# Half of the second gate's adaLN steps ahead of the second norm, their broadcast inside it, and three small first transfers on ScalarE's queue

## The chip, the core and the metric

The kernel runs on one core of one Trainium2 chip. A core has five engines, each with an instruction stream of its own that it works through in order: TensorE (PE in the profile; its weight loads are PEld), VectorE (DVE), ScalarE (ACT), GpSimd (POOL) and SyncE (SP). Transfers are started by an engine's queue and carried by 16 DMA engines. PE is granted one of two clocks, 1.2 or 2.4 GHz; the profile's PEclk is the granted share of the higher one. The metric is the time of one execution on the device in microseconds (us).

## What is computed

One layer of a hybrid decoder block on 256 tokens of width 2048 in float32. A conditioning vector c gives six modulation vectors (a shift, a scale and a gate for each half of the layer):

```python
c_act = jax.nn.silu(c)
mod = c_act @ w_ada[l] + b_ada[l]                   # (2048) x (2048, 6 * 2048)
sh1, sc1, g1, sh2, sc2, g2 = [...]                  # six pieces of 2048
xn = _rmsnorm(h, norm1_g[l]) * (1.0 + sc1) + sh1
proj = xn @ w_in[l]                                 # q, k, v, g_ret, conv gates, merge gates
y_ret = (retention(rotary(q), rotary(k), v) * jax.nn.silu(g_ret)) @ w_ret_o[l]
y_conv = (bg * _causal_dwconv(cg * xc, w_sc[l])) @ w_conv_o[l]
gate_a, gate_b = jnp.split(jax.nn.sigmoid(gate_logits + b_gate[l]), 2, axis=-1)
h = h + g1 * ((gate_a * y_ret + gate_b * y_conv) @ w_mix_o[l])
xn2 = _rmsnorm(h, norm2_g[l]) * (1.0 + sc2) + sh2
gt = _causal_dwconv(xn2 @ w_gate[l], w_ffconv[l], b_ffconv[l])
h = h + g2 * ((jax.nn.silu(gt) * (xn2 @ w_up[l])) @ w_down[l])
return _rmsnorm(h, final_g)
```

The gate g2 is used only at the very end of the layer, by the residual after w_down. The shift and scale of the second norm and the gate g1 are wanted before it.

## The kernel before

All weights stream from memory once, in tiles of 512 KB (256 rows x 512 columns). The program is one list of units, `units`, worked through by the loop at the end of `tile_trunk_block`. A unit has up to three steps, which the loop calls at different distances: `load` starts its transfer 9 units ahead (LOAD_AHEAD), `prep` runs 2 units ahead (PREP_AHEAD; 4 in the first stage), `run` issues its products. The kinds of unit:

- **Weights** (L285): `load` brings a raw tile (ring of 7, on SP's queue, L295); `prep` casts it to a rounded half `hi` on ACT (L307) and subtracts to get the low half `lo` on DVE (L308); in the first stage some go to tiles called `hw` and `lw`. `run` issues the products: three per tile and token half in `x_block` (activations stationary, L379 with hi, L380 with lo, L381 with hi), or in `w_block` (weights stationary) a 512-wide product with hi (L412) and a 256-wide one with lo (L417).
- **Ada** (L313): one step of adaLN, the product of c_act with w_ada, done on DVE and not on PE: `load` brings 512 KB of w_ada through the same raw ring, `prep` multiplies it by one number per partition and adds it to an accumulator `ada` (L342 the first of an accumulator, L344 the others). After 16 such steps half a modulation vector is summed but for the partitions; `done` sums them with a product with ones, and stores it.
- **Call** and **Loaded**: other work, and small loads with a step that uses them (the merge gates' bias among them, added at L706).

`spread` (L509) deals Ada units evenly among the Weights units of a stage. Which Ada units go where is set by counts: ADA_QK to each half of the q/k blocks, ADA_CONV0 to each half's convolution block, ADA_RET to w_ret_o, ADA_CONV to the later convolutions, ADA_OUT to w_conv_o, and what is left of `ada_mid` to w_mix_o. `ada_ff` holds the 32 steps of gate 2: 26 go to the first feed-forward blocks, 6 to the second block of the first w_down pass.

Order in time: the start (x's norm, its transposes L247 with copies L251, scales L358 to L370, first modulated activations L449 and L92) up to 32 us; the first stage, which interleaves chunks of xn and the first modulation, to about 400; q/k blocks, retention and the first convolution for two pairs of heads each, to 750; w_ret_o to 845; convolutions to 976; w_conv_o to 1075; w_mix_o to 1166; norm2 to 1178; the feed-forward blocks and w_down to the end.

A scheduler orders each engine's instructions; behind the first stage, DVE's L308 and L344 are held to the order of the program. `broadcast` (L541) turns half an accumulated gate into a tile of all partitions: two products of a matrix of ones with 512 columns each (L546), and two copies on ACT (L548). `norm2` (L882) ends the token norm: it sums the squares (L884), takes the root on POOL (L222), builds two diagonal tiles `dr` (L888), transposes the last quarter of h (`turn_h(3)`, L857, copies L860) and multiplies ones by the diagonals (L891).

## Time and profile before

| | us |
|---|---|
| median of 3 runs | 1919.06 (1918.51 to 1920.63) |
| the profiled execution, its own time | 1921.2 |
| its span | 1919.4 |
| PE busy | 1873.3 (98% of the span) |
| DVE busy | 1386.4 (72%) |
| ACT busy | 890.5 (46%) |
| mean granted clock of PE | 0.994 |

PE is busy nearly all the time, so the page's part 4 (the chain of work that ended last) lies on PE almost throughout. What is not PE's own work shows as its waits: in a timeline a row ends with the idle time before it and what ended that. Rows count the duration of each instruction; PE's products overlap one another, so in a row of products the time from one start to the next is what counts. A duration beside "x4" is that of the four together.

### The profile page before, as it was taken

The page shows a single profiled execution, that of the slowest core. Times are in us where ns is not written, and L with a number is a line of the kernel's source. Part 1 is how long each engine was busy: PE and PEld are TensorE (multiplying, and loading weights), DVE is VectorE, ACT ScalarE, POOL GpSimd, SP SyncE. Part 2 cuts the span into 40 slices and gives each one's busy share as a digit, 9 for nine tenths or more (in the row PEclk, how much of TensorE's full clock was granted, in tenths as well). Part 3 has the DMA queues.
Part 4 walks back from the last instruction along what each step waited for, and adds up shares of the span by engine and source line. Part 5 has one row for each costly group of instructions (what it writes and reads, how often), then busy time and mean ns, then how long its engine had stood idle before and what let it go on. Part 6 is the DMA issues. An engine that isn't in the chain of part 4 may idle for free.

```text
span 1919.4 us, 25328 instructions
## 1 busy us (share of the span) xinstructions
PE 1873.3 (98%) x9543; PEld 1579.5 (82%) x9543; DVE 1386.4 (72%) x1638; ACT 890.5 (46%) x1150; POOL 21.7 (1%) x51
## 2 busy tenths in 40 slices
PE   5999999999999999999999999999999999999997
PEld 5788888888888887888877787888888888888886
DVE  6799996766777787668777766877776556666665
ACT  4643434534444544344444445555554335555543
POOL 1000000000000000000000000000000000000000
PEclk9999999999999999999999999999999999999999
DMA  8989996566777676877777874777776756666553
GB/s 291 308 280 307 313 326 186 183 198 197 234 256 226 213 252 237 270 267 265 272 253 252 296 273 135 258 245 239 240 248 205 244 194 189 191 192 209 187 196 111
DMA packets 222093, 452.90 MB, mean 236 GB/s; under 512 B 14933, under 2 KB 27537, under 8 KB 221585
## 3 DMA queue, kind: packets, MB, share of 16 engines
q1 hardware_dynamic: 220768, 448.99, 70.8%
q10 hardware_dynamic: 720, 2.10, 0.3%
q8 instruction: 75, 1.23, 0.3%
q14 instruction: 50, 0.40, 0.1%
q0 software_dynamic: 480, 0.18, 0.0%
HBM read 449.11 MB, written 2.10 MB: 235 GB/s over the span
## 4 chain that ended last, share of the span: by engine, by line
PE 91%; DVE 4%; issue 2%; DMA 1%; ACT 1%; POOL 0%; SPq 0%; POOLq 0%; DVEq 0%; ACTq 0%
PE acc L412 30%; PE acc L417 15%; PE acc L380 15%; PE acc L381 14%; PE acc L379 14%; DVE lo L308 1%; PE misc L358 1%; DMA ld<-in_b_gate 1%; DMA raw<-in_w_ada 1%; PE misc L247 0%; DVE ada L344 0%; PE misc L546 0%; PE misc L632 0%; DVE conv L751 0%; ACT junk L228 0%
## 5 line engine op out<-in xcount | busy, mean ns | idle before, releaser
L307 ACT CAST hi<-raw 128x1024 fp32r<-128x1024 f32 (+1 forms) x601 | 623.9, 1038 | 862.8 <-PE acc L412 433.4
L308 DVE TENSOR_TENSOR lo<-raw,hi 128x1024 fp32r<-128x1024 f32 (+1 forms) x601 | 718.1, 1204 | 335.1 <-ACT hi L307 334.8
L412 PE MATMUL acc<-xn,hi 128*128 128x512 f32 x2688 | 840.6, 397 | 1.8 <-DVE xn L902 1.8
L417 PEld LDWEIGHTS acc<-xn,lo 128*128 128x128 f32 x2688 | 498.4, 188 | 124.2 <-DVE lo L308 10.1
L417 PE MATMUL acc<-xn,lo 128*128 128x256 f32 x2688 | 524.7, 279 | 3.6 <-DVE lo L308 3.3
L412 PEld LDWEIGHTS acc<-xn,hi 128*128 128x128 f32 x2688 | 414.7, 189 | 7.2 <-DVE xn L902 2.6
L344 DVE SCALAR_TENSOR_TENSOR ada<-raw,c_act,ada 128x1024 f32<-128x1024 f32 (+2 forms) x199 | 238.5, 1198 | 0.5
L379 PE MATMUL acc<-hi,ff_t 128*128 128x512 f32 x332 | 129.6, 390 | 0.0
L380 PE MATMUL acc<-lo,ff_t 128*128 128x512 f32 x332 | 129.3, 389 | 0.0
L381 PE MATMUL acc<-hi,ff_t 128*128 128x512 f32 x332 | 129.2, 389 | 0.0
L379 PE MATMUL acc<-hi,xn 128*128 128x512 f32 x304 | 119.5, 397 | 4.1 <-ACT xn L92 2.4
L380 PE MATMUL acc<-lo,xn 128*128 128x512 f32 x304 | 120.2, 395 | 1.1 <-DVE lo L308 1.1
L381 PE MATMUL acc<-hi,xn 128*128 128x512 f32 x304 | 119.5, 394 | 0.0
L381 PE MATMUL acc<-hw,xn 128*128 128x512 f32 x208 | 82.0, 394 | 0.0
L380 PE MATMUL acc<-lw,xn 128*128 128x512 f32 x208 | 81.8, 393 | 0.0
L379 PE MATMUL acc<-hw,xn 128*128 128x512 f32 x208 | 81.1, 395 | 0.0
L307 ACT CAST hw<-raw 128x1024 fp32r<-128x1024 f32 (+1 forms) x58 | 55.6, 959 | 45.0 <-DMA raw<-in_w_in 22.6
L423 ACT COPY sb<-acc 128x256 f32<-128x256 f32 x168 | 61.8, 368 | 30.9 <-PE acc L417 28.8
L380 PEld LDWEIGHTS acc<-lo,ff_t 128*128 128x128 f32 x332 | 62.3, 188 | 13.5 <-issue 0.2
L379 PEld LDWEIGHTS acc<-hi,ff_t 128*128 128x128 f32 x332 | 62.3, 188 | 13.0 <-ACT hi L307 0.2
L381 PEld LDWEIGHTS acc<-hi,ff_t 128*128 128x128 f32 x332 | 62.3, 188 | 12.9
L379 PEld LDWEIGHTS acc<-hi,xn 128*128 128x128 f32 x304 | 57.4, 189 | 17.8 <-ACT xn L92 2.4
(192 smaller groups left out, 1768.9 us busy)
## 6 DMA issues: line engine op xcount, KB each, us to landing
raw<-in_w_in SPq DMA_DIRECT2D x272, 512.0 KB, 4.8
raw<-in_w_ada SPq DMA_DIRECT2D x160, 512.0 KB, 4.9
raw<-in_w_gate SPq DMA_DIRECT2D x88, 512.0 KB, 4.3
raw<-in_w_up SPq DMA_DIRECT2D x88, 512.0 KB, 4.2
raw<-in_w_down SPq DMA_DIRECT2D x88, 512.0 KB, 4.4
raw<-in_w_ret_o SPq DMA_DIRECT2D x32, 512.0 KB, 5.3
raw<-in_w_conv_o SPq DMA_DIRECT2D x32, 512.0 KB, 5.5
raw<-in_w_mix_o SPq DMA_DIRECT2D x32, 512.0 KB, 5.5
```

Source lines behind the costliest of these rows:

```text
L307: nc.scalar.copy(self.hi, self.raw)
L308: in_order(nc.vector.tensor_tensor(self.lo, self.raw, self.hi.bitcast(F32), op=ALU.subtract))
L344: in_order(nc.vector.scalar_tensor_tensor(acc, self.raw[:, k], c_act[:, kt:kt + 1], acc, op0=ALU.mult, op1=ALU.add))
L358: nc.tensor.matmul(ps[:, i:i + 1], lhsT=flat[:, (s0 + i) * P:(s0 + i + 1) * P], rhs=ones[:, 0:1], start=True, stop=True,)
L379: nc.tensor.matmul(ps, lhsT=xh, rhs=u.hi[:, k, :], start=k0 + k == first, stop=False)
L380: nc.tensor.matmul(ps, lhsT=xh, rhs=u.lo[:, k, :], start=False, stop=False)
L381: nc.tensor.matmul(ps, lhsT=xl, rhs=u.hi[:, k, :], start=False, stop=k0 + k == end - 1)
L412: nc.tensor.matmul(ps, lhsT=u.hi[:, k, i * P:(i + 1) * P], rhs=xt(k0 + k).rearrange("p h s -> p (h s)"), start=k0 + k == 0, stop=False,)
L417: nc.tensor.matmul(ps[:, 0:S], lhsT=u.lo[:, k, i * P:(i + 1) * P], rhs=xt(k0 + k)[:, 0, :], start=False, stop=last and k == UK - 1,)
L423: nc.scalar.copy(b, ps[:, S:2 * S])
```

## The change

- The counts become 8, 12, 15, 28 and 14 instead of 6, 11, 13, 24 and 12, and `ada_mid` gets the 16 steps of gate 2's first half behind its 96: 97 of 112 are dealt before w_mix_o instead of 83 of 96, and 15 instead of 13 are left for w_mix_o.
- `ada_ff` keeps the 16 steps of the second half; all go to the first feed-forward blocks, none to w_down.
- When the first half is summed, `gate2_done` only keeps its accumulator; `norm2` issues its broadcast, behind the diagonal tiles and ahead of `turn_h(3)`, into two banks of the ring `acc` instead of `misc`.
- The three small transfers that stand first in the program (c, 8 KB; the positions, 128 KB to all partitions; the rotary frequencies, 0.5 KB) are started by ScalarE's queue instead of SyncE's. On ACT the first stands ahead of the table load, the others behind it; on SP the two 1 MB transfers of x are now first.

```diff
--- before.py
+++ after.py
@@ -38,7 +38,7 @@
 ROT_AT = 24
 DEFER_SG = 2
 ROT_EARLY = 12
-ADA_QK, ADA_CONV0, ADA_RET, ADA_CONV, ADA_OUT = 6, 11, 13, 24, 12
+ADA_QK, ADA_CONV0, ADA_RET, ADA_CONV, ADA_OUT = 8, 12, 15, 28, 14
 LAST_HEAD = 2
 NORM_AHEAD = 4
 
@@ -108,11 +108,11 @@
 
     x_tok = blk8("x_tok0", [P, D], F32), blk8("x_tok1", [P, D], F32)
     vec0 = w4("vec0", [P, P])
-    nc.sync.dma_start(vec0[0:16, :], c[0].rearrange("(r k) -> r k", k=P))
+    nc.scalar.dma_start(vec0[0:16, :], c[0].rearrange("(r k) -> r k", k=P))
     pos_i = small.tile([P, S], I32, tag="sb", name="pos_i")
-    nc.sync.dma_start(pos_i, positions.to_broadcast([P, S]))
+    nc.scalar.dma_start(pos_i, positions.to_broadcast([P, S]))
     ivf = const.tile([P, 1], F32, name="ivf")
-    nc.sync.dma_start(ivf, inv_freq)
+    nc.scalar.dma_start(ivf, inv_freq)
     for t in range(2):
         nc.sync.dma_start(x_tok[t], x[t * P:(t + 1) * P, :])
 
@@ -551,7 +551,9 @@
         return lambda acc: broadcast(acc, g1b, half, "g1b", misc_bank)
 
     def gate2_done(half):
-        return lambda acc: broadcast(acc, g2b, half, "g2b", misc_bank)
+        if half:
+            return lambda acc: broadcast(acc, g2b, 1, "g2b", misc_bank)
+        return lambda acc: g2b.update(acc=acc)
 
     def vec_done(which, half):
         def done(acc):
@@ -573,7 +575,8 @@
         ada_mid += ada_units(4, half, vec_done("scale", half))
     for half in range(2):
         ada_mid += ada_units(2, half, gate1_done(half), True)
-    ada_ff = [u for half in range(2) for u in ada_units(5, half, gate2_done(half), True)]
+    ada_mid += ada_units(5, 0, gate2_done(0), True)
+    ada_ff = ada_units(5, 1, gate2_done(1), True)
 
     def take(extra, n):
         got = extra[:n]
@@ -886,6 +889,7 @@
         dr = w4("dr", [P, 2, P])
         for t in range(2):
             nc.vector.tensor_scalar_mul(dr[:, t, :], ident, r[:, t:t + 1])
+        broadcast(g2b["acc"], g2b, 0, "g2b", acc_bank)
         turn_h(3)
         row["t"] = acc_bank()[:, 0:S]
         nc.tensor.matmul(row["t"], lhsT=ones, rhs=dr.rearrange("p t n -> p (t n)"), start=True, stop=True)
@@ -1023,7 +1027,7 @@
     for b0, b1_, final in ((0, cut, False), (cut, NB, True)):
         seq = [u for j in range(b0, b1_) for u in ff_blocks(j)]
         if not final:
-            seq = seq[:8] + spread(seq[8:], take(ada_ff, 26))
+            seq = seq[:8] + spread(seq[8:], take(ada_ff, 16))
             for k0 in range(KT - 2, NORM_AHEAD - 1, -2):
                 seq.insert((k0 - NORM_AHEAD) // 2 + 1, Call((lambda k: lambda: normed(k, k + 2))(k0)))
         units += seq
```

Lines of the changed kernel are 2 to 4 higher than those of before: L618 is L621, L860 is L863, L901 is L905.

How it moves instructions: on ACT in the first stage, where the last quarter of the second token half is copied (`x_t`), the first modulated activations are made (L449, `xn` at L92) and the first weights cast. Before:

```order
L251 COPY x_t_168<-misc_205 128x512
L251 COPY x_t_168<-misc_211 128x512
L307 CAST hi_304<-raw_268 128x1024
L449 ACTIVATE x_t_167<-x_t_167,b_218,a_217 128x256 x2
L92 CAST xn_29_221<-x_t_167 128x2x256
L307 CAST hw_316<-raw_282 128x1024
L307 CAST hi_339<-raw_302 128x1024
L480 COPY v_tok_225<-acc_352 128x512
L480 COPY v_tok_225<-acc_353 128x512
L307 CAST hw_348<-raw_311 128x1024
```

and now:

```order
L251 COPY x_t_168<-misc_205 128x512
L307 CAST hi_304<-raw_268 128x1024
L251 COPY x_t_168<-misc_211 128x512
L449 ACTIVATE x_t_167<-x_t_167,b_218,a_217 128x256 x2
L307 CAST hw_316<-raw_282 128x1024
L92 CAST xn_29_221<-x_t_167 128x2x256
L307 CAST hi_339<-raw_302 128x1024
L307 CAST hw_348<-raw_311 128x1024
L480 COPY v_tok_225<-acc_352 128x512
```

`hi_304` has moved ahead of the last copy of x_t, `hw_316` ahead of the cast of xn, and `hw_348` ahead of the first two copies of v_tok.

On DVE at the end of the first q/k block, where the four additions of the block's results (`qk`) stand; `lo_3510` before and `lo_3542` now are the low half of the next block's first unit. Before:

```order
L308 TENSOR_TENSOR lo_3464<-raw_3327,hi_3463 128x1024
L308 TENSOR_TENSOR lo_3486<-raw_3344,hi_3485 128x1024
L308 TENSOR_TENSOR lo_3510<-raw_3376,hi_3509 128x1024
L618 TENSOR_TENSOR qk_3519<-acc_3350,sb_3517 128x256
L618 TENSOR_TENSOR qk_3519<-acc_3351,sb_3525 128x256
L618 TENSOR_TENSOR qk_3519<-acc_3352,sb_3532 128x256
L618 TENSOR_TENSOR qk_3519<-acc_3353,sb_3539 128x256
L308 TENSOR_TENSOR lo_3545<-raw_3398,hi_3544 128x1024
```

and now:

```order
L308 TENSOR_TENSOR lo_3464<-raw_3327,hi_3463 128x1024
L308 TENSOR_TENSOR lo_3470<-raw_3344,hi_3469 128x1024
L344 SCALAR_TENSOR_TENSOR ada_3186<-raw_3376,c_act,ada_3186 128x1024
L621 TENSOR_TENSOR qk_3516<-acc_3350,sb_3514 128x256
L621 TENSOR_TENSOR qk_3516<-acc_3351,sb_3522 128x256
L621 TENSOR_TENSOR qk_3516<-acc_3352,sb_3529 128x256
L621 TENSOR_TENSOR qk_3516<-acc_3353,sb_3536 128x256
L308 TENSOR_TENSOR lo_3542<-raw_3398,hi_3541 128x1024
```

The adaLN step has taken the place of a unit of weights ahead of the additions, and the next block's first low half has come behind them.

On ACT in norm2, with the two last sums of squares (L228), the copies of the last quarter of h (`h_t`) and the first activations of the feed-forward stage. Before:

```order
L307 CAST hi_9945<-raw_9811 128x1024
L228 ACTIVATE junk_9852,ss_h<-h_tok_9072 128x512
L228 ACTIVATE junk_9863,ss_h<-h_tok_9074 128x512
L860 COPY h_t_9764<-misc_9877 128x512
L860 COPY h_t_9764<-misc_9883 128x512
L901 ACTIVATE xn_1948_9893<-u_9894,b_220 128x256
```

and now:

```order
L307 CAST hi_10003<-raw_9862 128x1024
L228 ACTIVATE junk_9903,ss_h<-h_tok_9123 128x512
L548 COPY g2b_9928<-acc_9929 128x512
L228 ACTIVATE junk_9914,ss_h<-h_tok_9125 128x512
L548 COPY g2b_9928<-acc_9932 128x512
L863 COPY h_t_9815<-misc_9935 128x512
L863 COPY h_t_9815<-misc_9941 128x512
L905 ACTIVATE xn_1968_9951<-u_9952,b_220 128x256
```

One copy of the broadcast (`g2b`) stands behind each of the two sums of squares, so the first of them ahead of the second sum, and both ahead of the copies of h.

## Rows read from the trace of the kernel before

**Rows 1.** Page, part 4: the chain that ended last, share by engine.

```profile
PE 91%; DVE 4%; issue 2%; DMA 1%; ACT 1%; POOL 0%; SPq 0%; POOLq 0%; DVEq 0%; ACTq 0%
```

**Rows 2.** PE's waits: line, what it waited for: us, times, longest.

```profile
PE acc L380 <- DVE lo L308: 5.3, 5, 2.6
PE acc L417 <- DVE lo L308: 3.3, 6, 1.2
```

**Rows 3.** Timeline of the start: start, us, engine, line, operation, tiles, count [idle].

```profile
0.74 0.39 SPq L111 DMA_DIRECT2D vec<-in_c  x1
...
2.12 0.91 SPq L117 DMA_DIRECT2D x_tok<-in_x  x2
...
2.60 0.25 PE L121 MATMUL misc<-ident,vec 16*128 16x16 f32 x1 [2.60 <-DMA vec<-in_c]
...
7.47 0.42 DVE L145 TENSOR_TENSOR rotary_room<-rotary_room,a_hi 128x256 f32<-128x256 f32 x1
...
9.44 0.63 ACT L228 ACTIVATE junk<-x_tok 128x512 bf16<-128x512 f32 x1 [6.12 <-DMA x_tok<-in_x]
...
12.92 0.49 DVE L342 TENSOR_SCALAR ada<-raw,c_act 128x512 f32<-128x512 f32 x1 [3.97 <-DMA raw<-in_w_ada]
...
19.21 9.07 PE L247 MATMUL misc<-diags,x_tok 128*128 128x128 f32 x56 [0.90 <-DVE diags L240]
...
28.32 0.59 ACT L251 COPY x_t<-misc 128x512 f32<-128x512 f32 x1 [0.35 <-PE misc L247]
...
28.81 1.05 ACT L307 CAST hi<-raw 128x1024 fp32r<-128x1024 f32 x1
...
31.54 0.61 DVE L342 TENSOR_SCALAR ada<-raw,c_act 128x768 f32<-128x768 f32 x1
...
32.37 0.79 PE L379 MATMUL acc<-hi,xn 128*128 128x512 f32 x1 [2.35 <-ACT xn L92]
```

**Rows 4.** Windows: busy us (x) PE, PEld, DVE, ACT, POOL; PEclk, DMA share, GB/s.

```profile
3.40:5.00 1.60, 0.00 (x0) 0.00 (x0) 0.12 (x1) 0.00 (x0) 1.60 (x4) 1.00 0.13 30
5.00:10.40 5.40, 0.00 (x0) 0.00 (x0) 2.40 (x8) 0.93 (x3) 2.08 (x5) 1.00 0.92 369
```

**Rows 5.** Timeline of PE at the first stage's waits, 48 to 52 us.

```profile
49.41 0.73 PE L379 MATMUL acc<-hi,xn 128*128 128x512 f32 x2 [0.49 <-ACT hi L307]
50.66 0.50 PE L380 MATMUL acc<-lo,xn 128*128 128x512 f32 x1 [0.53 <-DVE lo L308]
```

**Rows 6.** Timeline of PE and DVE where the first q/k block ends.

```profile
422.35 0.40 PE L417 MATMUL acc<-xn,lo 128*128 128x256 f32 x2
...
423.55 1.22 DVE L308 TENSOR_TENSOR lo<-raw,hi 128x1024 fp32r<-128x1024 f32 x1
```

**Rows 7.** Timeline of DVE and PE at the first two blocks of w_conv_o.

```profile
984.16 1.28 DVE L344 SCALAR_TENSOR_TENSOR ada<-raw,c_act,ada 128x1024 f32<-128x1024 f32 x1
...
984.30 0.50 PE L380 MATMUL acc<-lo,conv_t 128*128 128x512 f32 x1 [1.37 <-DVE lo L308]
...
1030.24 0.50 PE L380 MATMUL acc<-lo,conv_t 128*128 128x512 f32 x1
```

**Rows 8.** Timeline of PE at the entry to w_ret_o.

```profile
755.08 0.79 PE L380 MATMUL acc<-lo,y_t 128*128 128x512 f32 x1 [2.57 <-DVE lo L308]
```

**Rows 9.** Timeline of ACT and PE in norm2.

```profile
1167.71 0.63 ACT L228 ACTIVATE junk<-h_tok 128x512 bf16<-128x512 f32 x1
...
1170.20 0.70 PE L891 MATMUL acc<-dr,ones 128*128 128x256 f32 x2 [1.85 <-DVE dr L888]
```

**Rows 10.** Timeline of PE around the broadcast in the feed-forward stage.

```profile
1337.97 0.63 PE L412 MATMUL acc<-xn,hi 128*128 128x512 f32 x2
...
1338.67 0.63 PE L412 MATMUL acc<-xn,hi 128*128 128x512 f32 x2
1339.14 1.90 PE L546 MATMUL misc<-ada,ones 128*128 128x512 f32 x4
...
1341.12 0.62 PE L412 MATMUL acc<-xn,hi 128*128 128x512 f32 x2
```

## The prediction

> **What bounds the kernel now.** I read the chain that ended last first: 91% of the span is PE and 4% DVE [rows 1], so time comes and goes only where PE stands without work or does other work than the products. The list of PE's waits says where that is: five waits of x_block products for a low half `lo` (5.3 us) and six of the lo products of w_block (3.3 us, the longest 1.2) [rows 2]. All else is the start, in which PE's first weight product comes at 32.37 [rows 3], and norm2, where PE waits for what VectorE scales [rows 9]. So the reader takes the change place by place: the start, the hand-over of prepared weights, and the four places at which a multiply-add step of adaLN is put ahead of a `lo` that PE will need soon. One such step is 1.28 us of DVE [rows 7], with the next instruction starting 1.2 us after it.
>
> **The start (T1), +0.8.** Three small issues leave SP's queue: vec0 was issued at 0.74, x at 2.12 [rows 3], so x is issued 1.4 us earlier. The transfers gain more than that, by my reading: between 3.4 and 5.0 us the DMA engines were busy 13% of the time, and from 5.0 on 92% [rows 4]. In that lull x was already issued but waited, behind the small packets of the positions and the frequencies. The first small transfer, issued at 0.74, had landed and was worked on at 2.60 [rows 3], so a transfer that nothing stands ahead of begins some 1.2 us after its issue (my estimate from these two). Issued at 0.74, x starts at about 1.9 instead of 5.0: 3.1 us earlier, and the w_ada tile behind it likewise. Its first multiply (12.92) then starts at about 9.8 [rows 3]. From there to the 56 normalised transposes were 6.29 us (19.21 minus 12.92), and five rotary steps, which before stood ahead of that multiply, now stand behind it; one of them is 0.42 long itself (7.47), and since DVE starts the next before one ends I count 0.31 each, 1.55 in all [rows 3]. So of the 3.1 the 56 transposes keep 1.55. Three things are then late. The cast of `hi_304` stands ahead of the last x_t copy: 1.05, less the 0.35 for which ACT idled before that copy, +0.7. The first multiply of the next chunk (0.61) stands ahead of scale_of, +0.6. The cast of `hw_316` (again 1.05) stands ahead of the cast of xn for which the first product waits, +1.05 [rows 3]. Together −1.55 + 0.7 + 0.6 + 1.05 = +0.8. Bounds: −3.1, if neither the casts nor the rotary steps cost anything, and +2.5, if x only gains its issue time (1.7 less than assumed).
>
> The lull of [rows 4] speaks for a gain beyond the issue. The Trainium skill (DMA: Bandwidth & Descriptors, "Issuing engines are not separate DMA queues") says that transfers started by different engines end on the same 16 DMA engines and interleave, so that issuing from several saves only the sequencer's time. By that rule T1 would be +2.5 instead of +0.8; no run here shows yet which holds.
>
> **Weights prepared one unit earlier on ACT (T2), −2.5.** Before, two copies of v_tok stand ahead of `hw_348`; now none does, and the later hi casts stand one unit earlier among the copies. PE waited at 49.41 for a hi (0.49) and at 50.66 for its lo (0.53), and the products beside these waits ran 0.1 us longer each; the pair repeats once, at 62 [rows 5]. That is 1.25 us a place, two places, −2.5. ACT's cover is there, since each cast had stood behind a copy that itself waited for PE. Bounds: 0, if the raw tiles land no earlier than the casts began, and −2.5.
>
> **The ends of the q/k blocks (T3), +3.4.** Four times (pairs 0 to 3) an adaLN unit takes the place of a weights unit at a block's end, so that the `lo` of the next block's first unit falls behind the four additions that wait for PE. At the first place it would be done when 423.55 + 1.22 = 424.77 is reached, where PE's first product with that unit's low half stood at 422.35 [rows 6]. PE's order is changed too: eight hi products stand first instead of two, six more at about 0.23 us, 1.4 us. That leaves 424.77 − 423.75 = 1.0 us of waiting. At the second and fourth place the retention's steps stand beside it and waits of this form exist already [rows 2], so I take 0.85 each, +3.4. Bounds: 0, and 4 × 1.2, the longest wait of the form, +4.8.
>
> **The convolution, gates and first projection stages.** There the steps trade places one for one; a wait of the form [rows 2] vanishes in one block and comes in the next, with the same six or so hi products put ahead. I take 0, bounds −1.2 and +1.2.
>
> **Entry to w_conv_o and its second block (T6), +2.4.** At 984.30 PE had waited 1.37 for a lo, and the multiply-add came right behind that lo, at 984.16; now it stands ahead. The same at 1030.24, where PE has no wait now [rows 7]. Each costs one step, 1.2 us. The entry to w_ret_o, where the step already stood ahead, had a wait of 2.57 [rows 8], just 1.2 more than the 1.37. Bounds 0 to +2.4; what would cover it is a load landing late for another reason, and no row shows that.
>
> **norm2 (T7), +0.55.** Broadcasting half of gate 2 is four PE records of 1.90 us [rows 10], which begin right behind the last mix product, while PE waits for the last residual; PE waits 1.85 more behind it, before 1170.20 [rows 9]. The products are free. But on ACT one copy of 128x512 (0.59 [rows 3]) stands ahead of the second sum of squares (1167.71), and from there the path runs over r_h to the diagonal product at 1170.20. So +0.55. Bounds 0 and +1.2 (both copies).
>
> **The feed-forward stage (T8), −1.75.** At 1339.14 the same broadcast stood in a full PE: pairs of hi products follow each other at 0.70 us (1337.97, 1338.67), and the next came at 1341.12, 2.45 later: 1.75 us lost [rows 10]. That goes, with nothing in its place. The ten multiply-adds fewer in the stage, and six fewer in w_down, are DVE's alone and give nothing.
>
> **Sum**: 0.8 − 2.5 + 3.4 + 0 + 2.4 + 0.55 − 1.75 = +2.9. Against the profiled execution (1921.2 us, span 1919.4) that is 1924.1; this execution lies 2.1 us above the median of the three runs, 1919.06, and against that it is **1922.0**. A measurement of this kernel can tell about 0.2%, 3.8 us, from no change: below 1915.2 is faster, above 1922.9 slower.
>
> **The rivals.** *Faster*: the whole 3.1 us at the start carries through, because the casts find ACT idle, and the eight hi products cover the block ends. T1 is −3.1 and T3 is 0: 2.9 − 3.9 − 3.4 = −4.4, 1914.7. For it speaks that ACT idled before the last copy; against it that casts are placed right in front of what PE waits for [rows 3]. *Absorbed*: the start is as forecast, but T3 and T6 find cover: 2.9 − 3.4 − 2.4 = −2.9, 1916.2. Against it speaks the wait of 2.57 [rows 8], which shows one step at full price. *Slower*: x lands only 1.4 us earlier, since the small packets share the engines with it. Then T1 is +2.5, and the raw tiles behind it come later, so that only half of T2 is won: 2.9 + 1.7 + 1.25 = +5.9, 1924.9. It decides from a first sum of squares that starts after about 8.0 us, where I expect about 6.4 (before: 9.44 [rows 3]). For it speaks that the DMA engines are full from 5.0 us on [rows 4], so that nothing behind x can catch up. It is the time that the page's rule above would give.
>
> **How the numbers follow.** Forecast 0.42, of which 0.32 lies within 0.2% and 0.10 above it, since 1922.0 is close to that bound; absorbed 0.12, all within; faster 0.22; slower 0.24. So faster 0.22, same 0.44, slower 0.34. The forecast's own range, by half of T2 and half of T3, is 1920 to 1923.5. The range for 8 in 10 takes in the middles of both outer cases: 1914.0 to 1926.0.
>
> **What would show it.** In the profile after: PE's first product near 33.2 (below 31 is the faster case, above 34.5 the slower); no waits for hi and lo from 48 to 64; four waits of L417 of about 0.85 behind lo at 424, 475, 596 and 648; the wait at w_conv_o's entry 2.6 instead of 1.4 and a new one of 1.2 in its second block; the diagonal product of norm2 half a microsecond later against the last mix product; no broadcast near 1339. The prediction is wrong if DVE or ACT take the small shifts without PE noticing, or if a load (the gates' biases among them, which are now wanted earlier) lands behind its new place.

## The result

The changed kernel takes 1934.35 us (median of 4 runs, 1933.24 to 1939.31), the kernel before 1919.82 (4 runs, 1918.51 to 1920.63). The ratio is 1.0079, with a 95% interval of 1.0067 to 1.0091: it is slower by about 15 us. The forecast was 1922.0 with a range of 1914.0 to 1926.0. The profiled execution has a span of 1933.5 us, before 1919.4: the 14.1 us between the two are what the traces have to account for.

To see where they arise I took all products with weights (9120 in both traces), in order of time, and subtracted the start of each before from the start of the same-numbered one after. The difference, PE's lag, changes in steps (the ends of the stages are where their products end in the trace of before):

| stretch (times of before) | lag at its end, us | change | predicted |
|---|---|---|---|
| start, to the first product (32) | +3.1 | +3.1 | +0.8 |
| first stage, to 410 | −1.8 | −4.9 | −2.5 |
| q/k blocks, retention, first convolutions, to 746 | +5.7 | +7.5 | +3.4 |
| w_ret_o and the later convolutions, to 977 | +8.1 | +2.4 | 0 |
| w_conv_o, to 1071 | +18.9 | +10.7 | +2.4 |
| w_mix_o, to 1166 | +15.3 | −3.6 | 0 |
| norm2, to 1178 | +15.6 | +0.4 | +0.55 |
| feed-forward and w_down | +14.1 | −1.5 | −1.75 |

Two of these hold PE's own work that has only moved, the broadcasts of g1, of 1.7 to 2.0 us each: its first half is now made in the later convolutions, its second half in w_conv_o, which had the first half before, and w_mix_o has none. So some 1.8 of the 2.4 is no loss, and 2.0 of the 3.6 no gain; the other 1.6 of w_mix_o is a gain, with which a wait of 0.84 for h_tok at 1095.90 went. The 10.7 of w_conv_o is loss in full. The losses lie before norm2; the broadcast of g2, at norm2 and in the feed-forward stage, does what was forecast.

The list of PE's waits in the changed kernel, with line, what ended the wait, us in all, times and the longest (the rows of before are [rows 2]):

```profile
PE acc L380 <- DVE lo L308: 11.8, 5, 2.7
PE acc L417 <- DVE lo L308: 6.4, 8, 2.1
...
PE misc L358 <- DVE ada L344: 2.5, 1, 2.5
```

The waits for a low half of x_block have gone from 5.3 to 11.8 us, those of w_block from 3.3 to 6.4, and a wait of 2.5 for an adaLN step is new. They stand at two kinds of place, and the start is a third.

**The hand-overs in w_conv_o.** Four places of the first kind are here: the entry and the ends of the first three blocks. PE, ACT and DVE at the end of the first block, and PE's waits at the entry and in the second block:

```profile
993.64 0.50 PE L380 MATMUL acc<-lo,conv_t 128*128 128x512 f32 x1 [2.58 <-DVE lo L308]
...
1015.09 1.03 PE L806 MATMUL misc<-ident,gate_a 128*128 128x128 f32 x8
...
1015.88 0.72 PE L379 MATMUL acc<-hi,conv_t 128*128 128x512 f32 x2
1016.24 1.07 ACT L92 CAST mixed<-misc 128x512 fp32r<-128x512 f32 x2
1016.85 1.29 DVE L93 TENSOR_TENSOR mixed<-misc,mixed 128x512 fp32r<-128x512 f32 x2 [3.82 <-ACT mixed L92]
1018.05 1.22 DVE L308 TENSOR_TENSOR lo<-raw,hi 128x1024 fp32r<-128x1024 f32 x1
...
1019.32 0.53 PE L380 MATMUL acc<-lo,conv_t 128*128 128x512 f32 x1 [2.73 <-DVE lo L308]
...
1020.08 0.63 PE L379 MATMUL acc<-hi,conv_t 128*128 128x512 f32 x1
...
1020.50 0.63 PE L380 MATMUL acc<-lo,conv_t 128*128 128x512 f32 x1
...
1045.09 0.50 PE L380 MATMUL acc<-lo,conv_t 128*128 128x512 f32 x1 [1.22 <-DVE lo L308]
```

At the entry the wait is 2.58 where it was 1.37 [rows 7], and in the second block there is a wait of 1.22 where there was none; these two had been forecast. The wait of 2.73 at 1019.32, which comes once more at the end of the third block (1070.77), had not. It is read from the bottom: the low half that PE wants (lo, 1018.05) is queued on DVE behind the subtractions of `mixed` (1016.85), these wait for ACT's casts (1016.24), which wait for PE's own transposes of the gated sum (1015.09), which came behind the block's last product. Before, DVE had at this place:

```profile
1001.84 1.22 DVE L308 TENSOR_TENSOR lo<-raw,hi 128x1024 fp32r<-128x1024 f32 x1
...
1004.79 1.29 DVE L93 TENSOR_TENSOR mixed<-misc,mixed 128x512 fp32r<-128x512 f32 x2 [1.73 <-ACT mixed L92]
1006.00 1.22 DVE L308 TENSOR_TENSOR lo<-raw,hi 128x1024 fp32r<-128x1024 f32 x1
```

A low half stood ahead of the subtractions, so PE had a whole unit of products, some 2.7 us, to do while the sum went round the three engines; now an adaLN step has that place, and PE has two products.

The waits are not all of it: together they are 7.9 us longer than before, and the stage lost 10.7. Behind the two waits of 2.7 the granted clock of PE falls to 0.50, its lower level of 1.2 GHz (windows of the changed kernel, columns as in [rows 4]):

```profile
1019.65:1023.06 3.41, 3.41 (x9) 2.66 (x8) 3.09 (x3) 0.00 (x0) 0.00 (x0) 0.50 0.59 190
1070.85:1074.26 3.41, 3.41 (x7) 2.38 (x8) 3.33 (x3) 0.00 (x0) 0.00 (x0) 0.50 0.58 196
```

In these stretches a product starts every 0.42 us (1020.08, 1020.50), where at the full clock it is every 0.23, so that each costs PE some 1.4 us more, an estimate from the 2.8 that the waits leave over. With it a hand-over costs 4.1 to 4.3 us, of which 2.7 is waiting. Behind the wait of 2.58 at the entry the clock stays at 1.00, so the length of a wait alone does not tell whether it falls.

**The ends of the q/k blocks, and the columns of the second scale.** Two rows of PE:

```profile
423.06 1.22 PE L417 MATMUL acc<-xn,lo 128*128 128x256 f32 x8 [0.95 <-DVE lo L308]
...
699.48 1.95 PE L358 MATMUL misc<-ones,ada 128*128 128x1 f32 x16 [2.54 <-DVE ada L344]
```

The first is the first of four forecast waits; they are 0.95, 0.41, 0.93 and 2.12 long, 4.4 in all, where before only the last place had waits, of 0.60 and 0.40. The second was not forecast: 16 adaLN steps are now complete while the second retention ends, PE has their column products (L358) next in its queue, and the last step stands on DVE behind the retention's gating, 2.54 us late, where before PE had a wait of 1.19 (697.02). Behind the wait of 2.12 and behind the columns the granted clock is 0.50 for 3.4 us each, from 651.0 and from 702.2, where before it was 1.00. So the 7.5 us of the stretch are 3.4 and 1.35 of waits and some 2.7 of the lower clock. All four stretches together make some 5.5 of the 14.1 us; the mean granted clock was 0.990 to 0.991 in each of the four executions of the changed kernel, and 0.993 to 0.996 in those of the kernel before.

**The start.** ACT, DVE and PE at the same places as in [rows 3]:

```profile
6.18 0.63 ACT L228 ACTIVATE junk<-x_tok 128x512 bf16<-128x512 f32 x1 [1.00 <-DMA x_tok<-in_x]
...
10.41 0.29 DVE L145 CAST rotary_room<-pos_i 128x256 f32<-128x256 int32 x1 [5.02 <-DMA pos_i<-in_positions]
...
12.34 0.35 DVE L145 TENSOR_SCALAR rotary_room<-rotary_room,ivf 128x256 f32<-128x256 f32 x1 [1.64 <-DMA ivf<-in_inv_freq]
...
12.94 0.48 DVE L342 TENSOR_SCALAR ada<-raw,c_act 128x512 f32<-128x512 f32 x1
...
20.86 9.33 PE L247 MATMUL misc<-diags,x_tok 128*128 128x128 f32 x56 [0.64 <-DVE diags L240]
...
29.77 1.05 ACT L307 CAST hi<-raw 128x1024 fp32r<-128x1024 f32 x1
...
30.71 0.59 ACT L251 COPY x_t<-misc 128x512 f32<-128x512 f32 x1
...
33.90 1.03 ACT L307 CAST hw<-raw 128x1024 fp32r<-128x1024 f32 x1
34.84 0.61 ACT L92 CAST xn<-x_t 128x512 fp32r<-128x512 f32 x1
...
35.50 0.80 PE L379 MATMUL acc<-hi,xn 128*128 128x512 f32 x1 [3.83 <-ACT xn L92]
```

x landed earlier, as forecast: the first sum of squares stands at 6.18 instead of 9.44. But the first adaLN multiply stands at 12.94, where it stood at 12.92 before, and not at 9.8. The positions came at 10.41 and the frequencies at 12.34; before, these two rows were

```profile
5.20 0.29 DVE L145 CAST rotary_room<-pos_i 128x256 f32<-128x256 int32 x1 [1.68 <-DMA pos_i<-in_positions]
6.75 0.35 DVE L145 TENSOR_SCALAR rotary_room<-rotary_room,ivf 128x256 f32<-128x256 f32 x1 [1.26 <-DMA ivf<-in_inv_freq]
```

From the multiply to the 56 transposes it takes 7.92 us instead of 6.29, and from there 14.64 instead of 13.16, with the casts of hi and hw ahead of the copy and of xn. PE begins 3.1 us later. One execution differs from another here: with the transfers moved as in the change and the rotary steps left early, the first product stands at 34.2 to 35.5 us in five traces, with the old order at 31.4 to 32.4 in four, so the loss is some 2 to 4 us.

**norm2.** The broadcast on PE, the second sum of squares on ACT and the diagonal product on PE, to be read beside [rows 9]:

```profile
1181.08 1.88 PE L546 MATMUL acc<-ada,ones 128*128 128x512 f32 x4
...
1183.32 0.63 ACT L228 ACTIVATE junk<-h_tok 128x512 bf16<-128x512 f32 x1
...
1185.81 0.70 PE L895 MATMUL acc<-dr,ones 128*128 128x256 f32 x2 [1.97 <-DVE dr L891]
```

The broadcast takes 1.88 us behind the last mix product and is over before the path comes back to PE; only 0.4 us of lag shows, which fits ACT's copy ahead of the second sum.

### The profile page after: what moved, and what is told of

Its sections match the earlier page's. It is cut to its first block, busy times and chain, and to the rows that moved or that the text cites. A ratio compares the mean times of both kernels' runs of the same rounds, so it can differ in the third digit from the quotient of the medians.

```text
span 1933.5 us, 25321 instructions
## 1 busy us (share of the span) xinstructions
PE 1876.4 (97%) x9543; PEld 1584.8 (82%) x9543; DVE 1385.7 (72%) x1638; ACT 889.8 (46%) x1150; POOL 22.0 (1%) x51
## 4 chain that ended last, share of the span: by engine, by line
PE 62%; DVE 3%; issue 1%; DMA 1%; ACT 1%; POOL 0%; SPq 0%; POOLq 0%; DVEq 0%; ACTq 0%
PE acc L412 24%; PE acc L417 12%; PE acc L380 8%; PE acc L381 8%; PE acc L379 8%; DVE lo L308 1%; DVE ada L344 1%; DMA ld<-in_b_gate 0%; DMA raw<-in_w_conv_o 0%; PE misc L546 0%; PE misc L358 0%; ACT hi L307 0%; DMA raw<-in_w_ada 0%; DMA h_tok<-in_x 0%; ACT junk L228 0%
```

## The experiments

A ratio is against the kernel before, run on the same chip in the same session; the interval is that of 95%. The theory put to the test first: **what costs is the place of an adaLN step at a block's end on DVE, not the number of steps that are done before norm2, and not the first transfers.** Its rivals: the load of the steps on DVE and on the transfers, and a late start that pushes what follows. The diffs below show only the lines that do the work.

**The two halves of the change apart.** `first_only` is the kernel before with

```diff
-    nc.sync.dma_start(vec0[0:16, :], ...)    # and pos_i, ivf
+    nc.scalar.dma_start(vec0[0:16, :], ...)  # and pos_i, ivf
```

> Only the three first transfers go by ScalarE's queue; the adaLN steps stand as before. Theory (the orders at the start do two opposite things): PE's first product stays near 35.5 us (before 32.37), since the rotary steps that wait for the positions stand on VectorE ahead of the first adaLN multiply, and by 85 us PE has gained it back and is about 1.6 us ahead of before, since the weights are cast one unit earlier on ACT; from there all as before, so about 1.5 us faster, some 1918. Rival (the first stage's gain in the changed kernel has another cause, the moved adaLN steps): the 3 us at the start stay, about 1922.5.

Measured: 1919.58 us, ratio 0.9994 (0.9985 to 1.0003). In its trace the first product stands at 34.16, 1.8 us late, and PE is 2.6 us ahead of before at 77 us and 3.4 at 85: both halves of the theory, the late start and a gain of about 5 behind it. The gain does not come from the moved steps, which this kernel doesn't have. In all it makes no difference that these runs can tell; the profiled execution, 1917.56, is 2.0 below the kernel's own median.

`ada_only` is the changed kernel with these three lines put back.

> Only the adaLN steps and the broadcast move; the three first transfers stay on SyncE's queue. Theory: start and first stage as before, all else as in the changed kernel: 14.1 us of the two traces plus the 1.6 us that the start and first stage gave there, about 15.7 us slower than before, some 1935.5; five waits of x_block products for a low half of 11.8 us in all. Rival (the late start pushes the later transfers and so makes part of the later waits): clearly less than 14 us, some 1928.

Measured: 1936.39, ratio 1.0084 (1.0070 to 1.0097), 16.4 us above before and 2.0 above the changed kernel. The moved steps carry the whole loss; the lag grows in the same places as in the table, so a late start is not its cause.

**One count put back, and the same count changed alone.** `out12`:

```diff
-ADA_QK, ADA_CONV0, ADA_RET, ADA_CONV, ADA_OUT = 8, 12, 15, 28, 14
+ADA_QK, ADA_CONV0, ADA_RET, ADA_CONV, ADA_OUT = 8, 12, 15, 28, 12
```

> The changed kernel with 12 instead of 14 adaLN steps dealt to w_conv_o, two more left for w_mix_o: the low half of each next block stands again ahead of the two subtractions of the gated sum. Theory (the place of the step at the blocks' ends costs, not the number of steps): the two new waits of 2.7 us in w_conv_o go, and the 1.2 us each at its entry and second block, in all about 8 us: some 1926. Rival (the load of DVE and of the DMA queues with two more steps costs): 1 to 2 us back, some 1933.

Measured: 1925.37, ratio 1.0029 (1.0019 to 1.0039): 9.0 us less than the changed kernel, by two steps moved into w_mix_o. Its row for waits of x_block for a low half, columns as above:

```profile
PE acc L380 <- DVE lo L308: 4.2, 3, 2.6
```

11.8 us have become 4.2, less than before, and the granted clock is 1.00 all through w_conv_o. `out14_alone` is the counterpart, the kernel before with one number changed:

```diff
-ADA_QK, ADA_CONV0, ADA_RET, ADA_CONV, ADA_OUT = 6, 11, 13, 24, 12
+ADA_QK, ADA_CONV0, ADA_RET, ADA_CONV, ADA_OUT = 6, 11, 13, 24, 14
```

> The kernel before with 14 instead of 12 adaLN steps dealt to w_conv_o, nothing else. Theory: the whole loss of w_conv_o in the changed kernel appears alone, two new waits of 2.7 us for a low half and 1.2 us each at the entry and in the second block, some 8 us slower, 1927.5. Rival (these waits need the convolutions' changed counts too): within 2 us of before.

Measured: 1928.64, ratio 1.0051 (1.0036 to 1.0066), 8.3 us slower. Its row:

```profile
PE acc L380 <- DVE lo L308: 11.7, 6, 2.7
```

The entry and the ends of the first and the third block wait as in the changed kernel (2.59, 2.73 and 2.74), and the clock falls behind the last two as there; the wait of the second block, which the theory had too, does not come. By the two traces w_conv_o loses 9.4 us and w_mix_o gives 1.6 of them back. The clock goes with the count: from 977 to 1085 us the granted clock is 0.97 in all four traces with 14 steps (`after`, `ada_only`, `qk6`, `out14_alone`) and 1.00 in `before`, `first_only`, `out12` and `spread16`, which have 12. Two steps more in 36 units make over half of the change's loss, from either side. The sum of DVE's work in the stage can't do that: two steps are 2.4 us, on an engine that before was busy for 65.9 of the 90 us from 985 to 1075.

**The q/k blocks.** `qk8_alone`, again the kernel before with one number changed:

```diff
-ADA_QK, ADA_CONV0, ADA_RET, ADA_CONV, ADA_OUT = 6, 11, 13, 24, 12
+ADA_QK, ADA_CONV0, ADA_RET, ADA_CONV, ADA_OUT = 8, 11, 13, 24, 12
```

> The kernel before with 8 instead of 6 adaLN steps dealt to each half of the q/k blocks, nothing else (four fewer left for w_mix_o). Theory: the waits for a low half at the four block ends appear alone, about 1.0, 0.7, 1.1 and 1.6 us; the columns of the second scale, which PE makes when their last step is done, fall again near the end of the retention and cost 2 to 3 there: some 5 to 7 us slower, 1925.5. Rival (only the sum of steps in a stage counts): within 2 us of before.

Measured: 1926.03, ratio 1.0030 (1.0019 to 1.0041), 5.5 us slower, within what the theory gave. Its row for the waits of w_block:

```profile
PE acc L417 <- DVE lo L308: 7.9, 11, 2.1
```

7.9 us instead of 3.3, with 0.95, 0.41, 0.94 and 2.07 at the four block ends. The theory's second half missed: PE has no wait for the columns of the second scale (707.06). Instead there are more waits for low halves, of 0.4 to 1.0 each, and behind the columns of the first scale the granted clock is 0.50 from 545.9 to 549.3. `qk6` is the changed kernel with 6 in the first place:

```diff
-ADA_QK, ADA_CONV0, ADA_RET, ADA_CONV, ADA_OUT = 8, 12, 15, 28, 14
+ADA_QK, ADA_CONV0, ADA_RET, ADA_CONV, ADA_OUT = 6, 12, 15, 28, 14
```

> The changed kernel with 6 instead of 8 adaLN steps dealt to each half of the q/k blocks, four more left for w_mix_o. Theory: the first low half of the next block stands again ahead of the four additions, so the four waits at 422, 476, 596 and 650 us go, about 4.5 us, and the sum that PE waits for at 699 us falls elsewhere, another 2: some 1928. Rival (they are hidden by other waits behind them): 1 us, some 1933.

Measured: 1932.69 (4 runs, 1930.52 to 1936.48), ratio 1.0065 (1.0051 to 1.0079). By the median only 1.7 us come back, by the two profiled spans 4.8 (1928.7 to 1933.5). In its trace the four forecast waits and that for the adaLN step are gone; the ones of before at 649, 652 and 697 are back (0.51, 0.41 and 1.19), and one of 0.99 for column products at 810 is new, where the count of steps is now completed. So this run decides less than its counterpart: the waits go, and a part of the gain is spent behind them. Its four executions spread with the clock, from 1930.52 at a mean granted clock of 0.994, the profiled one, to 1936.48 at 0.991.

**16 steps ahead of norm2 without the bad places.** `spread16`, the changed kernel with

```diff
-ADA_QK, ADA_CONV0, ADA_RET, ADA_CONV, ADA_OUT = 8, 12, 15, 28, 14
+ADA_QK, ADA_CONV0, ADA_RET, ADA_CONV, ADA_OUT = 6, 11, 17, 32, 12
```

> The changed kernel with other counts: 6 and 11 as before for the q/k blocks and the first convolutions, 17 for w_ret_o, 32 for the later convolutions, 12 as before for w_conv_o, the rest (17) for w_mix_o. The 16 steps still stand ahead of norm2 and the broadcast within it. Theory (what costs is where a step stands at a block's end, not that 16 more steps are done before norm2): q/k blocks and w_conv_o as before, start and first stage 1.6 us ahead, feed-forward 1.7 gained, norm2 0.5 lost; the later convolutions may lose 1 to 3: some 1916 to 1920. Rival (16 more steps ahead of norm2 cost by their load on VectorE and on the transfers): 10 us slower than before, some 1929.

Measured: 1920.42, ratio 1.0002 (0.9994 to 1.0011), just above the 1916 to 1920 that the theory gave. The steps and the broadcast stand where the change wants them, 95 steps ahead of w_mix_o where the changed kernel has 97 and the one before 83, and 14 us of the loss are gone. The rival, their load, is out. What the move gains at the start and in the feed-forward stage it loses again, in waits of w_block for a low half: 5.2 us in all, where before had 3.3, the longest of 1.6 in a later convolution (897.01), with the granted clock at 0.50 from 896.7 to 900.1.

**Why the start was late.** My second theory: the first multiply has its data by 9.8 us and waits behind the rotary steps on DVE, which wait for the positions. `late_rot` is `first_only` with no rotary step at the start:

```diff
-ROT_EARLY = 12
+ROT_EARLY = 0
```

> The three first transfers by ScalarE's queue and all rotary steps issued late in the first stage, none at the start; the adaLN steps as before. Theory (in the changed kernel the first multiply waits behind the rotary steps, not for its own data): the first multiply starts near 9.8 instead of 12.9, the 56 transposes near 15, PE's first product near 30 (34.2 with the early rotary steps); with the gain of the first stage kept, about 4 to 5 us faster than before, some 1915. Rival (w_ada's data land late for another reason): first multiply near 12.5, first product near 33, some 1918.5.

Measured: 1918.98, ratio 0.9992 (0.9983 to 1.0000), but the theory fell. The row of the first multiply:

```profile
12.41 0.49 DVE L342 TENSOR_SCALAR ada<-raw,c_act 128x512 f32<-128x512 f32 x1 [7.55 <-DMA raw<-in_w_ada]
```

Nothing stands ahead of it now, and it waits for its own data until 12.41. The scheduler put three more adaLN steps in the place of the rotary ones, and the 56 transposes started at 20.57, the first product at 34.88. So x gained 3.8 us (its first sum stands at 5.68) and the tile behind it on the same queue 0.5. The windows of the first transfers (busy us of PE, PEld, DVE, ACT and POOL, granted clock, DMA share, GB/s), in the changed kernel:

```profile
1.60:4.00 2.40, 0.00 (x0) 0.00 (x0) 0.00 (x0) 1.08 (x2) 2.40 (x5) 1.00 0.79 232
4.00:6.00 2.00, 0.26 (x1) 0.18 (x1) 0.35 (x2) 0.22 (x1) 1.65 (x4) 1.00 0.99 410
6.00:8.00 2.00, 0.00 (x0) 0.00 (x0) 0.00 (x0) 1.75 (x5) 0.00 (x0) 1.00 0.76 288
8.00:10.00 2.00, 0.00 (x0) 0.00 (x0) 0.00 (x0) 1.13 (x4) 0.81 (x2) 1.00 0.68 231
10.00:12.00 2.00, 0.00 (x0) 0.00 (x0) 0.29 (x1) 1.63 (x5) 0.74 (x2) 1.00 0.86 276
```

and in the kernel before:

```profile
1.60:4.00 2.40, 0.25 (x1) 0.18 (x1) 0.35 (x2) 0.84 (x3) 2.40 (x5) 1.00 0.31 45
4.00:6.00 2.00, 0.00 (x0) 0.00 (x0) 0.29 (x1) 0.00 (x0) 1.67 (x4) 1.00 0.36 110
```

Before, the engines were little used from 1.6 to 6.0 us and full from then on (0.99 and more from 6 to 12); now they are well used first, and less than full, at 0.68 to 0.86, from 6 to 12. The stretch had not gone: it was shallower, and stood behind x's first half, around the first use of the positions (10.41). `start_mid` puts them between x's halves, with c on ScalarE's queue:

```diff
+    nc.sync.dma_start(x_tok[0], x[0:P, :])
     nc.sync.dma_start(pos_i, ...)
     nc.sync.dma_start(ivf, inv_freq)
-    for t in range(2): nc.sync.dma_start(x_tok[t], ...)
+    nc.sync.dma_start(x_tok[1], x[P:2 * P, :])
```

> The kernel before with only the start changed: c by ScalarE's queue, and on SyncE's queue the first half of x, the positions, the frequencies, the second half of x. ACT's order stays that of before (no weights cast ahead of the last copy of x_t or of xn). Theory: the rotary steps on VectorE wait for the positions only until about 8 us (10.4 and 12.3 in the changed kernel), the first adaLN multiply starts near 10.5 instead of 12.9, PE's first product near 31; the waits for hi and lo at 49 and 62 us stay, since they belong to ACT's order: about 1.3 us faster, some 1918.5. Rival (the gain of the first stage comes from transfers that start earlier): those waits go too, some 1914.

Measured: 1919.50, ratio 0.9997 (0.9989 to 1.0005). The first product stands at 31.26, and the waits of the first stage stayed, though PE starts 1.1 us earlier:

```profile
47.41 0.73 PE L379 MATMUL acc<-hi,xn 128*128 128x512 f32 x2 [0.47 <-ACT hi L307]
48.67 0.50 PE L380 MATMUL acc<-lo,xn 128*128 128x512 f32 x1 [0.53 <-DVE lo L308]
```

That speaks against the rival, by which the first stage's gain is from earlier transfers; `start_mid_casts2` below settles it. But the first multiply stands at 12.75 here too. `ivf_row` loads the frequencies as one row, a seventeenth beside c, instead of as 128 pieces of 4 bytes:

```diff
+    nc.sync.dma_start(vec0[16:17, :], inv_freq.rearrange("p o -> o p"))
-    nc.sync.dma_start(ivf, inv_freq)
-    c_raw = turned(vec0, 16, ...)
+    c_ivf = turned(vec0, 17, ...)
```

> The kernel before with one change: the 128 rotary frequencies come as one row of 512 bytes beside c (turned by the transpose that c has anyway) instead of as 128 pieces of 4 bytes; all three small transfers on SyncE's queue, orders of VectorE and ACT as before. Theory (the idle stretch of the DMA engines that stands at 3.4 to 5.0 us before, and moves behind x's first half when the small transfers go by ScalarE's queue, is the time of the 4-byte pieces on the same 16 engines): the stretch shortens by over 1 us, the first sum of squares starts near 8.0 instead of 9.4, w_ada's first tile is used near 11.5 instead of 12.9, PE's first product comes near 31 instead of 32.4; the waits at 49 and 62 us stay; 1 to 1.5 us faster, some 1918.5. Rival (the positions or the POOL queue's transfers make the stretch): start as before, within 0.3 us.

Measured: 1921.32, ratio 1.0003 (0.9994 to 1.0012). A miss: the first sum of squares stands at 9.70, the first product at 33.26, no earlier than before. The DMA engines are busier from 4 to 6 us (0.77 for 0.36), but at 0.14 from 1.6 to 4. `pos_row` takes the broadcast of the positions out of the transfers: one row of 1 KB, spread by a product with ones.

```diff
-    nc.sync.dma_start(pos_i, positions.to_broadcast([P, S]))
+    nc.sync.dma_start(pos_i[0:1, :], positions.to_broadcast([1, S]))
-        step(v.tensor_copy, a_lo, pos_i)
+        v.tensor_copy(row[0:1, :], pos_i[0:1, :])
+        nc.tensor.matmul(ps[:, 0:S], lhsT=ones[0:1, :], rhs=row[0:1, :], start=True, stop=True)
+        v.tensor_copy(a_lo, ps[:, 0:S])
```

> The kernel before with the positions loaded as one row of 1 KB and spread to the partitions by a product with ones on PE, instead of by a transfer of 128 KB that writes them to 128 partitions. Theory (the positions' transfer makes the stretch in which the DMA engines move little): the stretch between 1.6 and 5 us shortens, the first sum of squares starts near 7.5 instead of 9.4, w_ada's first tile is used near 11.2 instead of 12.9, PE's first product near 30.7; later all as before: some 1918.5. Rival (any transfer ahead of x on its queue costs a fixed time of this size): first sum of squares after 9, first product within 0.7 of 32.4, total as before, 1920.3.

Measured: 1918.14, ratio 0.9985 (0.9976 to 0.9994). The windows of `ivf_row` and then of `pos_row`, and the latter's first sum of squares, first multiply and first product:

```profile
1.60:4.00 2.40, 0.25 (x1) 0.17 (x1) 0.35 (x2) 0.84 (x3) 2.40 (x5) 1.00 0.14 32
4.00:6.00 2.00, 0.00 (x0) 0.00 (x0) 0.00 (x0) 0.00 (x0) 1.65 (x4) 1.00 0.77 202
```

```profile
1.60:4.00 2.40, 1.36 (x3) 0.67 (x3) 0.66 (x3) 0.84 (x3) 2.40 (x5) 1.00 0.46 69
4.00:6.00 2.00, 0.10 (x1) 0.00 (x0) 1.75 (x6) 0.00 (x0) 2.00 (x5) 1.00 0.94 385
```

```profile
7.03 0.63 ACT L235 ACTIVATE junk<-x_tok 128x512 bf16<-128x512 f32 x1 [3.83 <-DMA x_tok<-in_x]
...
11.29 0.49 DVE L349 TENSOR_SCALAR ada<-raw,c_act 128x512 f32<-128x512 f32 x1 [1.09 <-DMA raw<-in_w_ada]
...
30.37 0.80 PE L386 MATMUL acc<-hi,xn 128*128 128x512 f32 x1 [2.35 <-ACT xn L92]
```

From 4 us on the engines are full, and sum, multiply and product come 2.4, 1.6 and 2.0 us earlier than before. So, at the head of the queue, it was the transfer of the positions to 128 partitions that held up what is queued behind it. That it does so in its other places too is read from their windows, and no run tests it.

**Why the first stage gained.** Theory: the order of ACT alone, in which weights are cast ahead of the copies of v_tok and sg_tok. The hold, in `ivf_row_casts` (on `ivf_row`) and `start_mid_casts` (on `start_mid`), with `early` passing an instruction through the scheduler's own means of keeping the program's order, for the 58 instructions after the first:

```diff
-            nc.scalar.copy(self.hi, self.raw)
+            early(nc.scalar.copy(self.hi, self.raw))
-                nc.scalar.copy(d, ps)
+                early(nc.scalar.copy(d, ps))
```

> As ivf_row, and the casts of the first stage (all but the first) and the copies of v_tok, sg_tok and the gates held to the program's order on ACT, by which a cast stands ahead of the copies of the unit four before it. Theory (the first stage's gain of 4.6 us in the changed kernel is ACT's order alone): first product as in ivf_row, the waits at 49, 62 and 78 us go, some 4.5 us less than ivf_row: 1914. Rival (it needs the raw tiles that land earlier with the small transfers on ScalarE's queue): as ivf_row, 1918.5.

> As start_mid (c by ScalarE's queue, positions and frequencies between the two halves of x) with the same hold on the order of ACT's casts and copies as in ivf_row_casts. Theory: first product near 31.3, the waits at 48, 60 and 77 us go: about 4.5 us less than start_mid, some 1915. Rival: as start_mid, 1919.5.

Measured: 1920.61, ratio 1.0003 (0.9995 to 1.0012), and 1919.80, ratio 0.9996 (0.9987 to 1.0005). In both traces the waits near 48, 60 and 77 us are gone, and a new one has come with the hold, here in `start_mid_casts`:

```profile
73.62 1.28 PE L385 MATMUL acc<-hw,xn 128*128 128x512 f32 x2 [2.33 <-ACT gate_a L486]
```

The copies of a gate stand on ACT at 73.00, behind a cast (72.05) and behind activations that had waited 5.29 us for a scale (69.75), and PE waits for the bank that they empty; the granted clock is 0.50 from 73.0 to 79.9 us. So what the hold gained is lost again there. `start_mid_casts2` ends the hold before the gates' copies:

```diff
-        return tc.keep_in_program_order(ins) if 1 < seen[0] < 60 else ins
+        return tc.keep_in_program_order(ins) if 1 < seen[0] < 28 else ins
```

> As start_mid_casts (positions and frequencies between the halves of x), but the hold on ACT's order ends with the copies of v_tok and sg_tok, ahead of the gates'. Theory: first product near 31.3, the waits at 48 and 60 us gone, that at 77 left, no wait at 73: 3 to 4 us less than before, some 1916.5. Rival: within 1 us of before.

Measured: 1916.42, ratio 0.9973 (0.9964 to 0.9982). It differs from `start_mid` by this hold alone. From 30 to 70 us its trace has a single wait of PE, that for its first product:

```profile
31.03 0.50 PE L385 MATMUL acc<-hi,xn 128*128 128x512 f32 x1 [2.35 <-ACT xn L92]
```

`pos_ivf_casts` has the same hold and both rows (`ivf_row` and `pos_row`).

> Positions and frequencies as rows (pos_row and ivf_row together), and the casts and copies of the first two column groups held to the program's order on ACT. Theory: first product near 30.5, the waits at 48 and 60 us gone without a new one, 6 us faster in all: 1914.5. Rival (the order on ACT brings nothing by itself): 1918.

Measured: 1915.46, ratio 0.9974 (0.9964 to 0.9984). With first product at 30.34 and no waits at 48 and 60, it is faster than both kernels, by 0.26% against the one before, with the adaLN steps where they were.

## Why the prediction was wrong

**The step that failed most** is T6. It gave w_conv_o 2.4 us, one step each at the entry and in the second block, and left out the ends of the first and the third block, which so stood at nothing without a reason. The stage lost 10.7. The two places of T6 came as costed, 1.2 each. The other two cost 4.1 to 4.3 each: of the instructions ahead of the low half, the subtractions of `mixed` are not ready when DVE comes to them, since they wait for transposes and casts that begin with PE's last product, and the low half now stands behind them. `out14_alone` (8.3 slower) and `out12` (9.0 less) show it from either side, both net of what w_mix_o gives back.

**The clock** has no term in the prediction, which took PE's products at one rate throughout. Four stretches of 3.4 us at 0.50, two of them in w_conv_o and two in the q/k blocks and the retention, make some 5.5 us. The stages between, which the prediction put at 0 within 1.2 ("the steps trade places one for one"), came at 2.4, of which some 1.8 is the moved broadcast.

**T3**, the q/k blocks, was right in mechanism, and in the sum of the waits: 4.4 us less the 1.0 of before make 3.4, as forecast. That the sum fits is in part luck, since the places came at 0.95, 0.41, 0.93 and, less the 1.0 of before, 1.1, for a forecast of 0.85 each. `qk8_alone` has it alone, with what comes behind it, at 5.5. What was left out is the column product at the retention's end, 2.54 us for 1.19 before: I had read the moved steps on DVE only, not where the work falls that PE does when 16 of them are complete.

**T1**, the start, +0.8, was +3.1 in the two profiled executions (+1.8 in `first_only`). x's own gain was right to 0.2 us (6.18 for 6.4). The step that failed is "and the w_ada tile behind it likewise": I took the lull of [rows 4] as a time that x would escape, and didn't ask what the positions' transfer would hold up once x stood ahead of it. `late_rot` and `pos_row` show the answer: put on another engine's queue, the positions took 9.2 us from issue at 1.25 to use at 10.41, and the tile behind x gained 0.5 us, not 3.1 (12.41 in `late_rot`, 12.92 before). The Trainium skill (DMA: Bandwidth & Descriptors, "Issuing engines are not separate DMA queues") says that transfers started by different engines run on the same 16 DMA engines and interleave, and that starting them from several engines only saves the time of the issue. With the first half of this the traces agree, by these numbers; with the second they don't for x itself, which was issued 1.4 us earlier (0.74 for 2.12) and used 3.3 us earlier. The five rotary steps and the casts (1.6 and 1.5 us measured) were costed at 1.55 and 2.35; `late_rot` shows that the first of these is not the rotary steps as such, but whatever the scheduler puts between the first multiply and the second diagonal (8.2 us there, without them).

**T2**, −2.5, was −4.9, its mechanism right: the order on ACT alone does it (`start_mid` against `start_mid_casts2`). Beyond the two places that I counted, the wait for a copy at 79 us went too, 0.8 long, and PE had no wait from its first product to 82 us.

**T7 and T8**, the broadcast, were right: +0.4 for +0.55, and −1.75 at the broadcast's old place (1338 to 1341), as forecast, −1.5 over the whole stage. The rivals were all about the start or about cover at the block ends; none had a block end that gets worse than forecast, or a clock that falls, which is where the result was. The rival on the slow side, x gaining only its issue time, gives the start near what came (T1 +2.5), but by a mechanism that didn't happen: x itself gained over 3 us.

Three things stay open. The waits in `qk6` were not separated further. What exactly the positions' transfer waits for on the DMA engines is not shown by a profile that counts packets; only that with it the stretch comes and without it goes. And why the clock falls behind some waits (1.60 in `spread16`, 2.12 and 2.73 here) and not behind others (2.58 at the entry of w_conv_o) is not shown.

## What to carry to other kernels

A step that is dealt evenly among weight units costs little in most places (`spread16` has four more in w_ret_o than the kernel before, and PE's lag grows by 0.3 us there), up to its own time, 1.2 us, where a low half comes just in time, and a full round trip at a hand-over: where the next block's first low half stands behind an instruction that waits for PE's last product, PE stands until the result has gone round, 2.7 us here, and can then run at half its clock, another 1.4. So when a count changes, look at every block's end for what stands between the last operand PE can use and the first instruction that waits for PE, and compare what those instructions wait for, not how long they run. Read the granted clock behind each new wait as well, since a list of waits does not hold what it costs. And a transfer that is moved behind another still takes its share of the engines: ask what will now be late behind it.

## What was not expected of the hardware

Loading one row of 256 positions to 128 partitions, 128 KB, left the DMA engines little used at first (0.14 from 1.6 to 4 us in `ivf_row`, 0.31 in the kernel before) and held up the 2 MB and the weights queued behind it; with it on ScalarE's queue, a shallower hole stood behind x's first half (0.76, 0.68 and 0.86 from 6 to 12 us). Loaded as 1 KB and spread by one product with ones, the engines were at 0.94 from 4 us on and PE's first product came 2.0 us earlier. The 128 pieces of 4 bytes that I had suspected made no difference to x's first use or to the time.

Behind a wait of 2.7 us PE's granted clock was 0.50 for 3.4 us, and products started every 0.42 us instead of every 0.23.
